# Where the modulation sums, the gate chain and the spatial unit stand in a hybrid transformer layer's projection stage

## Chip, cores, metric

One core of one Trainium2 chip. The metric is the device time of one execution in microseconds (us). Three runs of the kernel before gave a median of 2624.97 us (2623.48 to 2627.48).

## What is computed

One layer on 2048 positions of width 1024, all in float32. Cut to what matters here:

```python
mod = silu(c) @ w_ada + b_ada            # six vectors of 1024
sh1, sc1, gt1, sh2, sc2, gt2 = split(mod)
h = rms_norm(x, g_mix) * (1 + sc1) + sh1
p = h @ w_in                             # q, k, v | qm, km, vm, om | u, v of the spatial unit | gates
y_attn  = forgetting_attention(...)      # 8 heads of 64, q and k normed per head
y_mlstm = mlstm_chunkwise(...)           # 4 heads, log-sigmoid forget gates
y_sgu   = gelu(u) * (tril(w_s) @ layer_norm(gelu(v)) + b_s)   # chunks of 128
x = x + gt1 * (concat(y) @ w_out)
x = x + gt2 * conv_ffn(rms_norm(x, g_ffn) * (1 + sc2) + sh2)
```

sh1 and sc1 are needed at once; sh2, sc2, gt1 and gt2 only when the projection stage is over.

## The kernel before

**Stages.** The projections (h @ w_in with what feeds attention and mLSTM) fill about the first 740 us. Attention, the output projection, and the up and down products of the channel network follow; the change does not touch them.

**Projection stage.** Two halves of 1024 positions, each with seven column blocks in this order: keys of mLSTM with the gates (272 columns), queries and output gates of mLSTM (512), values of mLSTM (256), spatial unit (512), k (512), q (512), v (512). Blocks of 512 columns are called wide (`wide[0]`). A block has eight results of 128 positions (of 512 in the second block, with the operands changed over). A result has eight k-steps, and a k-step three matmuls, since both operands are split in a high and a low part (`mm3`, L53 to L56). So a wide result is 24 matmuls of 512 columns on TensorE (PE).

**Ticks.** `products` (L598) issues the k-steps of a result and calls `tick` at its end, and in wide blocks also behind its fourth k-step. `tick` (L624) does what stands due: jobs that `after(n, f)` put off by n ticks; one step of `chores[0]`; one step of `background[0]`. The written order of these calls isn't quite that of the engines' queues: the layer that builds the program places each engine's instructions by estimates of its own, so the fences under the change show the order as it was built.

**Modulation sums.** `rest_of_mod` (L449), the only chore, makes the eight remaining column blocks of `mod` in 64 steps. A step multiplies a 128x512 tile of w_ada (`wa`) by a column of silu(c) and adds it to `modacc` on VectorE (DVE; L466 for the first of eight, L468 for the others). Its tile is loaded by a DMA on the queue of SyncE (SP), two steps ahead. The tiles lie in a ring of four buffers (tag t2k), which the bias row, the gate rows and h32 share. After the eighth step `columns_or_row` sums over partitions on PE, either by a matmul with 512 columns (L482) or by four with one column (L488), into the one bank of `misc_ps`. With a step at each tick from the second block on, the 64 steps are done in the k block of half 0.

**Weights.** The next block's eight weight tiles (`wr`, ring of four) are loaded on SP's queue and split by ScalarE (ACT, L592 for the high part) and DVE (L593 for the low part) during the present block.

**Gate chain.** `log_gates` (L796) turns the gates into logarithms: DVE, two activations on ACT (L803, L804, each behind a load of its function table), DVE (L805, L806). `rows(qi)` (L857), two for each half in the background, turns them over on PE (L868) and makes the rows that mLSTM and attention need.

**Spatial unit.** After four results of its block, `spatial` (L725) calls `mix(0)` to `mix(3)`, a matmul (L732) and two operations of DVE (L733, L734) each, two a tick, and then `turn(0)` and `turn(1)`, four transpositions each (L741). Their results go by turns to the one bank of `misc_ps` (called mp in the profile) and to the ring of two banks of `tr_ps` (trp). Also in mp: the key transpositions of mLSTM (L960, copied by ACT at L962) and the modulation sums (L482, L488). Also in trp: the transpositions of q and k (L781), and of h (L557).

**k and q.** `use_qk` squares a result on ACT, sums on DVE (L767, L768), takes the reciprocal root on GpSimd (POOL, L128), scales on DVE (L773) and turns over on PE three ticks later (L781).

Of the kernel before, what the change touches and what calls it, by code (L numbers as in the profile page):

```python
# [33 lines left out]
def trunk(  # L34
# [337 lines left out]
    def tr_ps():  # L372
        return pp.tile([P, 512], F32, name="trp", tag="trp")
# [75 lines left out]
    def rest_of_mod():  # L449

        seq = [(col, k) for col in (3072, 3584, 4096, 4608, 2048, 2560, 5120, 5632) for k in range(KT)]
        tiles = {}

        def load(i):
            if i < len(seq):
                col, k = seq[i]
                tiles[i] = pool.tile([P, 512], F32, name="wa", tag="t2k")
                dma(tiles[i], w_ada[k * P : k * P + P, col : col + 512])

        load(0)  # L460
        load(1)
        for i, (col, k) in enumerate(seq):
            st = tiles.pop(i)
            if k == 0:
                acc = pool.tile([P, 512], F32, name="modacc", tag="macc")
                V.tensor_scalar(acc, st, cs[:, 0:1], None, op0=ALU.mult)  # L466
            else:
                V.scalar_tensor_tensor(acc, st, cs[:, k : k + 1], acc, op0=ALU.mult, op1=ALU.add)  # L468
            load(i + 2)
            if k == 6:  # L470
                brow = pool.tile([1, 512], F32, name="brow", tag="t2k")
                dma(brow, b_ada[:, col : col + 512])
            if k == 7:
                V.tensor_tensor(acc[0:1, :], acc[0:1, :], brow, op=ALU.add)
                after(2, lambda acc=acc, col=col: columns_or_row(acc, col))
            yield
# [90 lines left out]
    class Weights:  # L567
# [7 lines left out]
        def load(self):  # L575
            k = len(self.raw)
            if k == KT:
                return
            raw = pool.tile([P, 512], F32, name="wr", tag=self.tags[k])
            o = 0  # L580
            for col, wd in self.parts:
                dma(raw[:, o : o + wd], w_in[k * P : (k + 1) * P, col : col + wd])
                o += wd
            self.raw.append(raw[:, : self.width])
# [13 lines left out]
    def products(i, mm):  # L598

        w = nxt[0]  # L600
        for k in range(KT):
            mm(k)
            if k == 3 and wide[0]:
                tick()
            if w and i == 7:
                if k in (0, 1, 2, 5):
                    w.cast()
                if k in (0, 1):
                    w.load()
        if w and 1 <= i <= 3:  # L610
            w.load()
        if w and 4 <= i <= 6:
            w.cast()
            w.load()
        tick()
# [4 lines left out]
    chores, started = [], []  # L620
    background = []
    ticks = [0]

    def tick():  # L624
        ticks[0] += 1
        due()
        if chores and started and next(chores[0], True):
            chores.pop(0)
        if background and next(background[0], True):
            background.pop(0)  # L630
# [15 lines left out]
    def after(n, f):  # L646

        pending.append((ticks[0] + n, f))
# [76 lines left out]
    def spatial(tt, u, vn):  # L725
        y = pool.tile([P, 4, 256], F32, name="sy", tag="t4k")

        def mix(g):
            sl = slice(g * 64, g * 64 + 64)
            mp = (misc_ps, tr_ps)[g % 2]()  # L730
            m3 = mp[:, 0:256].rearrange("p (n c) -> p n c", n=4)
            T.matmul(m3, wT[:, g, :], vn[:, :, sl], start=True, stop=True)  # L732
            V.tensor_tensor(y[:, :, sl], m3, bc(gsgu[:, sl], 1, 4), op=ALU.mult)  # L733
            V.scalar_tensor_tensor(  # L734
                y[:, :, sl], y[:, :, sl], bs_col[:, g : g + 1], u[:, :, sl], op0=ALU.add, op1=ALU.mult
            )

        def turn(j):
            mp = (misc_ps, tr_ps)[j % 2]()
            for n in range(4):  # L740
                T.transpose(mp[:, n * P : (n + 1) * P], y[:, n, j * P : (j + 1) * P], ident)  # L741
            t5 = pool.tile([P, 512], F32, name="evq", tag="sq")
            A.copy(t5, mp)
            dma(yt_d[768 + j * P : 896 + j * P, (tt - 3) * P : (tt + 1) * P], t5)

        for g in range(4):
            after(g // 2 + 1, lambda g=g: mix(g))
        for j in range(2):
            after(j + 4, lambda j=j: turn(j))
# [105 lines left out]
    cols = {}  # L855

    def rows(qi):  # L857
        t0 = qi * 512
        neb = nebs[qi % 2]
        ra = pool.tile([P, 512], F32, name="ra", tag="ra")  # L860
        rb = pool.tile([P, 512], F32, name="rb", tag="rb")
        r4 = lambda t: t.rearrange("p (n l) -> p n l", l=P)

        psG = mps()
        g = gates[:, qi // 2].rearrange("p a n h -> p (a n h)")
        for i in range(4):
            o = (qi % 2 * 4 + i) * 4
            T.transpose(psG[0:100, i * P : (i + 1) * P], g[:, o : o + 100], ident)  # L868
        psI = psG[64:68, :]
        m, e, lf = ra[0:4], ra[32:36], ra[64:68]  # L870
        b, a, ne = rb[0:4], rb[32:36], rb[64:68]
        V.tensor_copy(lf, psG[96:100, :])
        mp_ = pool.tile([36, 5], F32, name="mprev", tag="mprev")[32:36]
        V.tensor_copy(mp_[:, 0:1], mcar)
        yield
        V.tensor_tensor_scan(m, lf, psI, mcar, op0=ALU.add, op1=ALU.max)
        V.tensor_tensor_scan(b, rmask, lf, 0.0, op0=ALU.mult, op1=ALU.add)
        V.tensor_copy(mp_[:, 1:5], r4(m)[:, :, P - 1])
        V.tensor_copy(mcar, mp_[:, 4:5])
        yield  # L880
        V.tensor_tensor(a, psI, b, op=ALU.subtract)
        V.tensor_tensor(e, m, b, op=ALU.subtract)
        V.tensor_scalar(R[32:36], m, -1.0, None, op0=ALU.mult)
        V.tensor_copy(R[96:100], a)
        yield
        V.tensor_tensor(r4(R[0:4]), bc(mp_[:, 0:4], 2, P), r4(e), op=ALU.subtract)
        V.tensor_tensor(r4(R[64:68]), r4(a), r4(e)[:, :, P - 1 : P].broadcast_to([4, 4, P]), op=ALU.subtract)
        V.tensor_tensor(dec[0:4], mp_[:, 0:4], r4(e)[:, :, P - 1], op=ALU.subtract)
        yield
        fr = pool.tile([P, 512], F32, name="fr", tag="macc")  # L890
        for r in (0, 32):
            V.tensor_tensor_scan(
                fr[r : r + 4], ones[r : r + 4, 0:1].broadcast_to([4, 512]), psG[r : r + 4, :], fc[r : r + 4],
                op0=ALU.mult, op1=ALU.add,
            )
            V.tensor_copy(fc[r : r + 4], fr[r : r + 4, 511:512])
            dma(nf_d[r // 8 : r // 8 + 4, t0 : t0 + 512], fr[r : r + 4])
        yield
        psR = mps()
        for i in range(4):  # L900
            T.transpose(psR[:, i * P : i * P + 100], R[0:100, i * P : (i + 1) * P], ident[0:100, 0:100])
        psD = misc_ps()
        for pr in range(2):
            T.matmul(psD[:, pr * 4 : pr * 4 + 4], sel[:, pr, :], dec, start=True, stop=True)
        V.tensor_scalar(neb[32:36], e, -1.0, None, op0=ALU.mult)
        V.scalar_tensor_tensor(ne, e, -1.0, neb[32:36], op0=ALU.mult, op1=ALU.subtract)
        yield
        psR4 = psR.rearrange("p (n l) -> p n l", l=P)
        ecol = pool.tile([P, 4, 68], F32, name="ecol", tag="ecol")
        A.activation(ecol, psR4[:, :, 0:68], AF.Exp)  # L910
        acol = pool.tile([P, 4, 4], F32, name="acol", tag="acol")
        V.tensor_copy(acol, psR4[:, :, 96:100])
        dcol = pool.tile([P, 2, 4], F32, name="dcol", tag="dcol")
        A.activation(dcol.rearrange("p a b -> p (a b)"), psD[:, 0:8], AF.Exp)
        V.tensor_copy(neb[64:68], ne)
        V.tensor_tensor(neb[96:100], ne, neb[64:68], op=ALU.subtract)
        cols[qi] = ecol, acol, dcol
# [264 lines left out]
    class Block:  # L1182
# [10 lines left out]
        def mm(self, i, nb):  # L1193
            if i not in self.x:
                self.x[i] = pool.tile([P, D], F32, name="x2")
                dma(self.x[i], x[self.rows(i), :])
                self.st[i] = pool.tile([P, 2], F32, name="st", tag="wst_")
            sl = slice(i * P, (i + 1) * P)
            ps = self.ps[i, nb] = pp.tile([P, 512], F32, name="wps")
            for k in range(KT):  # L1200
                mm3(ps, self.y[k][0][:, sl], self.y[k][1][:, sl], *wo[nb * 8 + k], k == 0, k == KT - 1)
# [534 lines left out]
```

## Time and profile before

| | us |
|---|---|
| median of the runs | 2624.97 |
| the profiled execution's own time | 2626.13 |
| its span in the trace | 2624.1 |
| PE busy | 2537.4 (97%) |
| DVE busy | 2004.4 (76%) |
| ACT busy | 1274.2 (49%) |
| PE's granted clock, mean | 0.992 |

A row of the waits gives the engine, the operation that waited, what it waited for, the total in us, how often, and the longest. A row of a timeline gives start, duration, engine, line, operation, tiles, shape, and in brackets the idle time in front of it with what ended it. A row of the stretches gives from:to, length, busy us of PE, of PE's weight loads, DVE, ACT and POOL (with the number of instructions), PE's granted clock, the share of the DMA engines and GB/s. A group row has count, busy time and mean ns, and behind the last bar the idle time before the group's instructions.

### The profile page before, as it was taken

What the parts mean: (1) busy time and instruction counts of PE and PEld (TensorE: products, weight loads), DVE (VectorE), ACT (ScalarE), POOL (GpSimd) and SP (SyncE); (2) the same over time, 40 slices, a digit from 0 to 9 for tenths busy, and PEclk for the clock granted to TensorE, in tenths of its full rate; (3) what the DMA queues carried; (4) which work ended last, traced back from release to release, by engine and by line L of the source; (5) the groups of instructions that cost most, each with busy time, mean ns of one, the idle gap of its engine ahead of it and who ended that gap; (6) DMA issues with size and microseconds to landing.
All of it is one profiled execution on the core that took longest, in us unless ns stands there. A gap on an engine that the chain in (4) does not pass through costs nothing.

```text
span 2624.1 us, 36472 instructions
## 1 busy us (share of the span) xinstructions
PE 2537.4 (97%) x12521; PEld 2101.5 (80%) x12537; DVE 2004.4 (76%) x3438; ACT 1274.2 (49%) x2424; POOL 399.0 (15%) x532
## 2 busy tenths in 40 slices
PE   5999999999999999999989999999999999999999
PEld 4887878878787887777768888888888888888787
DVE  7856646455378888866769888888888887898797
ACT  4333334333278888854555444444444444444443
POOL 2012210032246656620000000000000000000000
PEclk9999999999999999999999999999999999999999
DMA  7564653334564445257723222246222227658533
GB/s 248 173 185 132 194 153 111 116 88 131 165 177 113 114 136 165 65 162 238 274 65 105 89 81 84 86 160 225 81 88 81 87 66 256 233 166 295 186 95 117
DMA packets 302592, 379.58 MB, mean 145 GB/s; under 512 B 31934, under 2 KB 194588, under 8 KB 300360
## 3 DMA queue, kind: packets, MB, share of 16 engines
q1 hardware_dynamic: 302408, 377.26, 45.4%
q8 instruction: 99, 1.62, 0.3%
q14 instruction: 85, 0.70, 0.1%
HBM read 276.44 MB, written 100.74 MB: 144 GB/s over the span
## 4 chain that ended last, share of the span: by engine, by line
PE 76%; DVE 10%; DMA 5%; ACT 3%; issue 3%; POOL 2%; SPq 1%; DVEq 0%; ACTq 0%; POOLq 0%
PE ub L56 10%; PE ub L55 10%; PE ub L54 10%; PE acc L54 5%; PE acc L56 5%; PE acc L55 5%; PE db L55 4%; PE db L56 4%; PE db L54 4%; PE sp L206 3%; PE tp L259 3%; PE wps L55 2%; PE wps L54 2%; PE wps L56 2%; PE op L245 2%
## 5 line engine op out<-in xcount | busy, mean ns | idle before, releaser
L54 PE MATMUL acc<-wh,hh 128*128 128x512 f32 (+2 forms) x768 | 288.2, 376 | 4.3 <-DVE ev L688 2.3
L54 PE MATMUL ub<-T,wsph 128*128 128x512 f32 x704 | 274.2, 390 | 5.8 <-ACT wsph L1348 5.8
L56 PE MATMUL acc<-wh,hl 128*128 128x512 f32 (+2 forms) x768 | 275.7, 362 | 0.8 <-DVE hl L563 0.5
L55 PE MATMUL acc<-wl,hh 128*128 128x512 f32 (+2 forms) x768 | 275.3, 360 | 0.3 <-DVE wl L593 0.3
L56 PE MATMUL ub<-T,wspl 128*128 128x512 f32 x704 | 273.7, 389 | 0.6 <-DVE wspl L1349 0.6
L55 PE MATMUL ub<-T,wsph 128*128 128x512 f32 x704 | 273.9, 389 | 0.0
L55 PE MATMUL db<-wspl,wsph 128*128 128x512 f32 x616 | 240.2, 390 | 2.6 <-DVE wspl L1480 2.6
L56 PE MATMUL db<-wsph,wspl 128*128 128x512 f32 x616 | 239.6, 389 | 0.0
L54 PE MATMUL db<-wsph 128*128 128x512 f32 x616 | 238.2, 389 | 0.3 <-ACT wsph L1479 0.3
L1348 ACT CAST wsph<-S 128x512 fp32r<-128x512 f32 x176 | 109.7, 623 | 227.7 <-PE ub L55 159.1
L263 DVE TENSOR_TENSOR plo<-tp,phi 128x512 fp32r<-128x512 f32 (+1 forms) x320 | 186.9, 607 | 31.6 <-ACT phi L262 29.4
L54 PE MATMUL ub<-B,wsph 128*128 128x512 f32 x528 | 207.1, 392 | 2.8 <-ACT wsph L1348 2.8
L56 PE MATMUL ub<-B,wspl 128*128 128x512 f32 x528 | 207.0, 392 | 0.7 <-DVE wspl L1349 0.7
L55 PE MATMUL ub<-B,wsph 128*128 128x512 f32 x528 | 206.8, 392 | 0.0
L223 ACT ACTIVATE L<-L,nm 128x1024 f32<-128x1024 f32 (+2 forms) x192 | 172.5, 902 | 35.7 <-DVE nm L212 34.4
L259 PE MATMUL tp<-ident,L 128*128 128x128 f32 x1088 | 177.0, 274 | 2.6 <-POOL L L228 0.8
L262 ACT CAST phi<-tp 128x512 fp32r<-128x512 f32 (+1 forms) x320 | 159.9, 520 | 40.5 <-PE tp L259 38.9
L206 PE MATMUL sp<-kk,q 128*128 128x512 f32 (+3 forms) x640 | 169.3, 375 | 3.2 <-DVE nm L212 2.2
L1479 ACT CAST wsph<-act 128x512 fp32r<-128x512 f32 x132 | 82.2, 623 | 178.9 <-PE db L55 161.0
L228 POOL TENSOR_SCALAR L<-L,rs 128x1024 f32<-128x1024 f32 (+2 forms) x192 | 167.2, 880 | 11.0
L54 PEld LDWEIGHTS acc<-wh,hh 128*128 128x128 f32 x768 | 147.1, 192 | 24.2 <-DVE ev L688 2.7
L56 PEld LDWEIGHTS acc<-wh,hl 128*128 128x128 f32 x768 | 146.0, 191 | 23.1 <-DVE hl L563 1.3
(339 smaller groups left out, 5936.2 us busy)
## 6 DMA issues: line engine op xcount, KB each, us to landing
w<-in_w_up_dram SPq DMA_DIRECT2D x88, 512.0 KB
wd<-in_w_down_dram SPq DMA_DIRECT2D x176, 256.0 KB
wa<-in_w_ada_dram SPq DMA_DIRECT2D x96, 256.0 KB
act_d<-yc SPq DMA_DIRECT2D x44, 512.0 KB
act<-act_d SPq DMA_DIRECT2D x44, 512.0 KB
wr<-in_w_in_dram SPq DMA_DIRECT2D x64, 256.0 KB
q<-q_d SPq DMA_DIRECT2D x128, 128.0 KB
hc_d<-hl SPq DMA_DIRECT2D x28, 512.0 KB
```

Of the source, the lines that this page charges most:

```text
L54: T.matmul(ps, lh, rh, start=start, stop=False, skip_group_check=resume)
L55: T.matmul(ps, lh, rl, start=False, stop=False, skip_group_check=resume)
L56: T.matmul(ps, ll, rh, start=False, stop=stop, skip_group_check=resume)
L206: T.matmul(sp[:, b : b + bw], q2[n][:, qs], kk[:, s0 + b : s0 + b + bw], start=n == 0, stop=n == 1 and not last)
L223: A.activation(L[c], L[c], AF.Exp, bias=nm[:, n - 1 : n], scale=-1.0, accum_out=rs[:, c : c + 1])
L228: G.tensor_scalar(t, t, rs[:, 0:1], 1.0, op0=ALU.mult, op1=ALU.mult)
L245: T.matmul(op[:, c0:], vv[:, j, :], hi[:, c0:], start=(j == 0), stop=False)
L259: T.transpose(tp[:, i * P : (i + 1) * P], rows[i][j // 8][:, (j % 8) * P : (j % 8 + 1) * P], ident)
L262: A.copy(hi[:, c0:], tp[:, c0:])
L263: V.tensor_tensor(lo[:, c0:], tp[:, c0:], hi[:, c0:].bitcast(F32), op=ALU.subtract)
L1348: A.copy(hi, src)
L1479: A.copy(hi, v)
```

## The change

Four parts. (1) The sums advance only at the tick in the middle of a wide result: one step a result instead of two, none in narrow blocks, so that the 64 steps end in the k block of half 1. Their tiles are loaded one step ahead instead of two. (2) The next block's first four weight tiles are loaded from result 0 on instead of from result 1, and one load of the last result falls away. (3) `rows(0)` and `rows(2)`, the first of each half, begin two ticks later. (4) `mix` and `turn` take all banks from `tr_ps`.

```diff
         load(0)
-        load(1)
         for i, (col, k) in enumerate(seq):
...
-            load(i + 2)
+            load(i + 1)
...
             if k == 3 and wide[0]:
-                tick()
+                tick(True)
             if w and i == 7:
                 if k in (0, 1, 2, 5):
                     w.cast()
-                if k in (0, 1):
+                if k == 0:
                     w.load()
-        if w and 1 <= i <= 3:
+        if w and i <= 3:
             w.load()
...
-    def tick():
+    def tick(middle=False):
         ticks[0] += 1
         due()
-        if chores and started and next(chores[0], True):
+        if middle and chores and started and next(chores[0], True):
             chores.pop(0)
...
         def mix(g):
-            mp = (misc_ps, tr_ps)[g % 2]()
+            mp = tr_ps()
...
         def turn(j):
-            mp = (misc_ps, tr_ps)[j % 2]()
+            mp = tr_ps()
...
     def rows(qi):
+        if qi % 2 == 0:
+            yield
+            yield
```

Line numbers in the changed kernel are one less than before from L462 to L856 and two more behind that.

PE's queue around the first transposition of the gates (L868, in the changed kernel L870), second block of half 0. acc_985 is the bank of the block's first result, the next acc that of the second; hh_480 belongs to the fourth of the eight k-steps, hh_524 to the last. Before:

```order
L54 MATMUL acc_985<-hh_524,wh_973 128x512
L868 MATMUL mps_1008<-ident_74,gates_85 100x128 x4
L55 MATMUL acc_985<-hl_525,wh_973 128x512
L56 MATMUL acc_985<-hh_524,wl_974 128x512
L54 MATMUL acc_1038<-hh_447,wh_839 128x512
```

Of the change:

```order
L54 MATMUL acc_1021<-hh_480,wh_929 128x512
L55 MATMUL acc_1021<-hl_481,wh_929 128x512
L56 MATMUL acc_1021<-hh_480,wl_930 128x512
L870 MATMUL mps_1039<-ident_74,gates_85 100x128 x4
L54 MATMUL acc_1021<-hh_491,wh_939 128x512
```

The transposition stood in the last k-step of the first result and stands behind the fourth k-step of the second, 14 matmuls later. In half 1 it moves by 24.

DVE's queue at the beginning of the k block of half 1, where the spatial unit's second group of four results is mixed (sy is its result; mp and trp are the banks; L767 to L773 belong to k's norm). Before:

```order
L767 TENSOR_REDUCE ss_5770<-qsq_5768 128x8
L768 TENSOR_SCALAR ss_5770<-ss_5770 128x8
L773 TENSOR_TENSOR qn_5788<-acc_5722,ss_5770 128x512
L733 TENSOR_TENSOR sy_5787<-mp_5804,gsgu_279 128x4x64
L767 TENSOR_REDUCE ss_5833<-qsq_5831 128x8
L734 TENSOR_SCALAR sy_5787<-sy_5787,colA_86,su_5485 128x4x64
L733 TENSOR_TENSOR sy_5787<-trp_5808,gsgu_279 128x4x64
```

Of the change:

```order
L467 TENSOR_SCALAR modacc_5708<-wa_5710,cs_92,modacc_5708 128x512
L766 TENSOR_REDUCE ss_5745<-qsq_5743 128x8
L767 TENSOR_SCALAR ss_5745<-ss_5745 128x8
L772 TENSOR_TENSOR qn_5763<-acc_5686,ss_5745 128x512
L467 TENSOR_SCALAR modacc_5708<-wa_5766,cs_92,modacc_5708 128x512
L467 TENSOR_SCALAR modacc_5708<-wa_5839,cs_92,modacc_5708 128x512
L467 TENSOR_SCALAR modacc_5708<-wa_5917,cs_92,modacc_5708 128x512
L467 TENSOR_SCALAR modacc_5708<-wa_6008,cs_92,modacc_5708 128x512
L732 TENSOR_TENSOR sy_5762<-trp_5782,gsgu_279 128x4x64
L766 TENSOR_REDUCE ss_5811<-qsq_5809 128x8
L733 TENSOR_SCALAR sy_5762<-sy_5762,colA_86,su_5439 128x4x64
L732 TENSOR_TENSOR sy_5762<-trp_5786,gsgu_279 128x4x64
```

Four sums have come between the scaled k and the first mix. At the same place of half 0 four sums stood there before, and three stand there now.

PE's queue in the spatial unit's block of half 0, where mLSTM's scores begin (mps is the bank of the scores). Before:

```order
L56 MATMUL acc_1745<-wh_1741,hl_525 128x512
L981 MATMUL mps_1801<-qz0_295,kT_1736 128x256
L488 MATMUL mp_1790<-ones_83,modacc_1440 128x1 x4
L981 MATMUL mps_1801<-qz0_295,kT_1736 128x256
L983 MATMUL mps_1802<-Cst_320,qT_1665 128x130 x2
```

Of the change:

```order
L56 MATMUL acc_1681<-wh_1677,hl_525 128x512
L983 MATMUL mps_1730<-qz0_295,kT_1672 128x256 x2
L985 MATMUL mps_1731<-Cst_320,qT_1607 128x130 x2
L54 MATMUL acc_1751<-wh_1530,hh_447 128x512
L55 MATMUL acc_1751<-wl_1531,hh_447 128x512
```

The sum's four matmuls into mp no longer stand there.

## Prediction

> **What bounds the kernel now.** The page's busy line, its row of granted clock and its chain of waits come first.
>
> ```profile
> PE 2537.4 (97%) x12521; PEld 2101.5 (80%) x12537; DVE 2004.4 (76%) x3438; ACT 1274.2 (49%) x2424; POOL 399.0 (15%) x532
> PE 76%; DVE 10%; DMA 5%; ACT 3%; issue 3%; POOL 2%; SPq 1%; DVEq 0%; ACTq 0%; POOLq 0%
> ```
>
> TensorE (PE) is busy for 2537.4 of 2624.1 us, so nothing in VectorE (DVE), ScalarE (ACT) or the queues counts unless PE stops for it. The change adds and removes no matmul. It can only move the time in which PE stands idle, or runs slowly, in the projection stage (0 to about 740 us). So the second view is PE's own waits in that stage; these rows lie where the change can reach (us in total, times, longest).
>
> ```profile
> PE mps L868 <- DVE gates L806: 5.2, 2, 2.8
> PE mp L732 <- DVE sy L733: 4.7, 1, 4.7
> PE mp L960 <- DVE sy L733: 3.1, 2, 2.8
> ...
> PE trp L557 <- ACT h L561: 3.0, 1, 3.0
> PE acc L54 <- DVE ev L688: 2.3, 2, 1.3
> ...
> PE mp L488 <- ACT kT L962: 2.0, 1, 2.0
> ...
> PE acc L55 <- DVE wl L593: 0.3, 1, 0.3
> ```
>
> That is 20.6 us in ten waits, 0.8% of the kernel: a ceiling of what idle time alone can give back. PE's timeline says where they are and what follows them (start, duration, matmul, idle time before it). I call the places A to F.
>
> ```profile
> 82.09 0.39 PE L54 MATMUL acc<-hh,wh 128*128 128x512 f32 x1
> 85.28 0.81 PE L868 MATMUL mps<-ident,gates 128*100 128x128 f32 x4 [2.80 <-DVE gates L806]
> ...
> 86.74 0.63 PE L54 MATMUL acc<-hh,wh 128*128 128x512 f32 x1
> 87.16 0.63 PE L55 MATMUL acc<-hl,wh 128*128 128x512 f32 x1
> ...
> 165.31 1.05 PE L488 MATMUL mp<-ones,modacc 128*128 128x1 f32 x8 [1.97 <-ACT kT L962]
> ...
> 238.00 0.39 PE L55 MATMUL acc<-wl,hh 128*128 128x512 f32 x1
> 238.23 0.39 PE L56 MATMUL acc<-wh,hl 128*128 128x512 f32 x1
> 243.29 1.22 PE L732 MATMUL mp<-sv,wT 128*128 128x256 f32 x2 [4.68 <-DVE sy L733]
> ...
> 394.16 0.66 PE L557 MATMUL trp<-ident,xt 128*128 128x128 f32 x4 [3.01 <-ACT h L561]
> ...
> 432.55 0.64 PE L868 MATMUL mps<-ident,gates 128*100 128x128 f32 x4 [2.41 <-DVE gates L806]
> ...
> 577.24 0.59 PE L732 MATMUL mp<-sv,wT 128*128 128x256 f32 x2
> ...
> 581.32 0.69 PE L960 MATMUL mp<-ident,kn 128*128 128x128 f32 x2 [2.83 <-DVE sy L733]
> ```
>
> A is 85.28, B 165.31, C 243.29, D 394.16, E 432.55, F 581.32. Look at the starts: before C two matmuls lie 0.23 us apart, behind A they lie 0.42 us apart. PE runs at about half speed after a wait, so a wait costs more than its idle time. The stretches give the price (length, busy times, granted clock, DMA share, GB/s):
>
> ```profile
> 85.00:90.00 5.00, 4.72 (x16) 3.87 (x17) 4.59 (x9) 1.04 (x3) 0.00 (x0) 0.66 0.45 136
> 165.00:170.00 5.00, 4.69 (x22) 4.04 (x23) 3.55 (x10) 2.70 (x5) 0.00 (x0) 0.75 0.26 81
> 170.00:175.00 5.00, 5.00 (x28) 4.30 (x27) 3.01 (x11) 0.00 (x0) 2.59 (x3) 0.90 0.74 236
> 243.00:250.00 7.00, 6.46 (x17) 4.73 (x18) 6.89 (x16) 0.37 (x1) 1.80 (x1) 0.54 0.50 167
> 394.00:404.00 10.00, 9.84 (x79) 9.66 (x80) 9.86 (x22) 8.56 (x17) 0.00 (x0) 1.00 0.75 244
> 434.00:444.00 10.00, 10.00 (x39) 8.06 (x39) 9.71 (x17) 1.20 (x2) 0.00 (x0) 0.84 0.19 60
> 580.00:590.00 10.00, 8.62 (x32) 7.03 (x34) 3.65 (x8) 3.37 (x6) 1.01 (x2) 0.66 0.13 35
> ```
>
> Lost to the clock, as (1 - clock) times length: A 0.34 x 5 = 1.7 us; B 0.25 x 5 + 0.10 x 5 = 1.75; C 0.46 x 7 = 3.2; D none; E 0.16 x 10 = 1.6; F 0.34 x 10 = 3.4, of which I take 2.6, since 1.3 us of the wait lie in the window. With its wait each place costs: A 4.5, B 3.7, C 4.7 + 0.25 + 3.2 = 8.1, D 3.0, E 4.0, F 5.4. Together 28.7 us.
>
> The Trainium skill, page "TensorE: Matmul & The Clock Gate", section "Part 1: The HAM clock gate", says that the clock halves after at least one idle window of about 3.4 us, and that the windows run freely. By that rule only C's 4.68 us would surely cost clock, and the sum below would be 5.05 us smaller (A, B and E without their 1.7, 1.75 and 1.6). The trace speaks against it: slow matmuls follow waits of 1.97 and 2.80 us, and none follow D's 3.01.
>
> **The change part by part.**
>
> *Gate chain later (A and E).* L868 turns the gates over after DVE's L806, which ends this chain:
>
> ```profile
> 80.87 0.75 ACT L592 CAST wh<-wr 128x256 fp32r<-128x256 f32 x2 [2.96 <-DMA wr<-in_w_in_dram]
> 81.64 1.28 ACT L803 ACT_TABLE_LOAD   x1
> ...
> 84.89 0.22 DVE L805 TENSOR_TENSOR gates<-lg,lg 128x64 f32<-128x64 f32 x1 [1.90 <-ACT lg L804]
> ```
>
> The order moves L868 in half 0 from behind the first matmul of the last k-step of a result to the middle of the next: 14 matmuls later, 14 x 0.227 = 3.2 us against the wait of 2.80. A goes: -4.5. If the chain itself slides by a cast (0.4 us), nothing changes; if the sums now ahead of it on DVE add two operations of 0.75, 1.1 us stay and the clock may with them (-1.7). In half 1 it moves 24 matmuls, 5.4 us against 2.41; the sums that now stand near L805 cost about 2.2 us (three of 0.75), and 5.4 still covers 4.6: -4.0. Bound: 0, if a sum waits for its tile there.
>
> *Sums at half rate (B).* L488 at B needs the one bank mp, which waits for L962's copy on ACT. In the new order no sum's matmul stands between the key transposes and the score matmuls there, and the other L488 and L482 have the bank free for many matmuls: -3.7. Bounds -3.7 and 0 (the score matmul L981 reads the same copy, so it may wait in its place).
>
> *Spatial unit in transposition banks, with the sums beside it (C and F).* Mixes 0 and 1 take the two trp banks, mixes 2 and 3 need them back, so now mix 2 waits for L733 of mix 0, and mix 3 for L733 of mix 1. DVE's rows at C and F:
>
> ```profile
> 236.15 0.69 DVE L773 TENSOR_TENSOR qn<-acc,ss 128x512 f32<-128x512 f32 x1 [1.75 <-POOL ss L128]
> 238.44 2.33 DVE L468 SCALAR_TENSOR_TENSOR modacc<-wa,cs,modacc 128x512 f32<-128x512 f32 x3 [1.60 <-DMA wa<-in_w_ada_dram]
> 242.15 0.75 DVE L468 SCALAR_TENSOR_TENSOR modacc<-wa,cs,modacc 128x512 f32<-128x512 f32 x1 [1.39 <-DMA wa<-in_w_ada_dram]
> 242.82 0.42 DVE L733 TENSOR_TENSOR sy<-mp,gsgu 128x256 f32<-128x256 f32 x1
> ...
> 575.86 0.69 DVE L773 TENSOR_TENSOR qn<-acc,ss 128x512 f32<-128x512 f32 x1 [1.75 <-POOL ss L128]
> 576.47 0.41 DVE L733 TENSOR_TENSOR sy<-mp,gsgu 128x256 f32<-128x256 f32 x1
> ```
>
> At C four sums stand between L773 (done 236.84) and L733, two of them late by their DMA. After the change three stand there. Three take 2.33; with one late tile of 1.60, L733 runs from 240.8 to 241.2. PE is ready at 243.29 - 4.68 = 238.6: mix 2 waits 2.6. L733 of mix 1 comes behind one L767 (0.68), one L734 (0.43) and itself (0.41), at 242.7, and mix 3 waits 1.1 more. So 3.7 us idle where 4.93 were. For the clock I take 2.4, in proportion (3.2 x 3.7 / 4.93): 6.1 against 8.1, or -2.0. Bounds: -8.1 if no wait is left, +2 with two late tiles.
>
> F has no sums before the change. After it, four stand between L773 (done 576.55) and L733: 4 x 0.777 = 3.1, so L733 ends at 580.1. Mix 2 is due at 577.24 and waits 2.8; mix 3 waits 1.1: 3.9 against 2.83, the clock as before: +1.1. L960 has bank mp to itself and waits no more. I take no late tile: there are four buffers, and the first of these sums stands ahead of L767 in the new order, so that the fifth tile can be on its way some 5 us (573.2 to 578.9, three sums behind L773) before it is needed. Bounds -5.4, and +2 x 1.6 more with two late tiles: +4.3.
>
> *Weights one result sooner.* The waits of PE for weights are 0.3 us in all, and those for the eviction L688, held behind casts, 2.3 in two: -1.0 (bounds -1.3, and +2.0 if the earlier load holds up a sum's tile on the one DMA queue, SP's, by 1.6). At D one matmul of a sum, about 0.9 us, now stands where PE was idle, and has left another place: -0.9 (0 to -3.0).
>
> *Sums in new places.* Forty of the 64 steps now run in half 0's q and v and half 1's blocks. This group row tells what they cost DVE:
>
> ```profile
> L468 DVE SCALAR_TENSOR_TENSOR modacc<-wa,cs,modacc 128x512 f32<-128x512 f32 x55 | 41.2, 749 | 16.0 <-DMA wa<-in_w_ada_dram 14.9 <-DVE modacc L468 0.3
> ```
>
> They waited 14.9 us for tiles and only at C did PE notice. I take +1.5, one small new wait (0 to +8).
>
> **Sum:** -4.5 - 4.0 - 3.7 - 2.0 + 1.1 - 1.0 - 0.9 + 1.5 = -13.5. The profiled execution took 2626.13 us (span and 2.03 around it): 2612.6. The median of the runs shown, 2624.97, lies 1.2 lower, so the median forecast is 2624.97 - 13.5 = 2611.5. The rivals are taken from the median too.
>
> **The rivals.** *All waits go:* if DVE reaches L733 in time at C and F as well, A, B, C, E and F go whole, and D and the weights by 1.9: 25.7 + 1.9 = 27.6 less, or 2597.4; with half a place and one small new wait left (2.0 + 1.5), about 2601. For it: at F L733 of mix 0 is in time today. Against: the order puts sums there.
>
> *The waits move:* the sums in half 1 hold L805 and E stays (+4.0), C and F each get one more late tile with its clock (+2.4 and +1.6), B's bank wait passes to L981 for half its price (+1.9): -13.5 + 9.9 = -3.6, or 2621.4. For it: L468 waits for tiles today with two loads ahead. Against: at half rate one load ahead is the same time, 24 x 0.227 = 5.4 us, as two at full rate.
>
> *Slower, by late tiles ahead of reads:* DVE works in order, so a sum that waits for its tile holds every read of a PSUM bank behind it. Each such place costs a wait of 1.6 and some 2.0 of clock, 3.6. The trace shows it at C with two tiles; if it happened at six places in the wide blocks of half 1, where no sum stood, it gives -13.5 + 6 x 3.6 = +8.1: 2633.1. It decides for slower by over 0.2% from about 5.2 places on (18.7 / 3.6). For it: four buffers are shared with other users. Against: of the sums in the group row above, all but the two at C held nobody.
>
> *It does nothing at L868:* if the chain of logs moves with it, A and E stay (+8.5): -5.0, or 2620.0.
>
> **How the numbers follow.** Forecast (2605 to 2619) 0.51; all waits go 0.14; the waits move, or L868 keeps them, 0.20; slower 0.15. A measurement of this kernel tells about 0.2%, 5.2 us, from no change, so the third case counts as same: faster 0.65, same 0.20, slower 0.15. The range, 2600 to 2630, leaves out about 0.05 below and 0.13 above.
>
> **What would show it.** Right: no wait of L868 for L806, no wait of L488 for L962, clock 1.00 around these; at C and F waits of 2 to 4 us on L733 under trp and none under mp. Wrong: DVE waits of L468 for wa ahead of L805 or L733 in half 1, new slow stretches in half 1, or slow clock without waits.

## The result and the profile after

| | before | after |
|---|---|---|
| median, us (22 runs each) | 2625.25 (2618.39 to 2628.99) | 2620.31 (2615.23 to 2625.63) |
| ratio | | 0.9982, 95% interval 0.9974 to 0.9989 |
| span of the profiled execution | 2624.1 | 2622.1 |

The change makes the kernel 4.9 us faster, 0.18%. The forecast was 13.5 us: right in sign, but not in size. Two rivals' numbers, 2621.4 (the waits move) and 2620.0 (L868 keeps its waits), lie close to the measured 2620.31, but neither tells what happened: both left a gate wait standing, and both are gone.

The waits of PE (TensorE) in the projection stage of the changed kernel, the rows that answer to those of before:

```profile
PE trp L731 <- DVE sy L732: 7.4, 2, 4.0
...
PE mps L985 <- ACT M L940: 4.6, 1, 4.6
...
PE mp L506 <- DVE colC L507: 2.7, 1, 2.7
...
PE trp L556 <- ACT h L560: 0.9, 1, 0.9
```

The two waits for the gates are gone, and so are those of the evictions, of the casts and of bank mp (L488 and L960). Two rows are new: L985, mLSTM's second group of scores, waits 4.6 us for its decay rows (M), and L506, a transposition in `small_setup`, waits 2.7 us for DVE's copy L507. The timeline has the places:

```profile
86.49 0.60 PE L870 MATMUL mps<-ident,gates 128*100 128x128 f32 x4
...
160.43 1.24 PE L985 MATMUL mps<-Cst,qT 128*128 128x130 f32 x4 [4.56 <-ACT M L940]
...
235.72 2.54 PE L731 MATMUL trp<-sv,wT 128*128 128x256 f32 x4 [3.38 <-DVE sy L732]
...
384.89 1.33 PE L556 MATMUL trp<-ident,xt 128*128 128x128 f32 x8 [0.85 <-ACT h L560]
...
493.08 0.30 PE L506 MATMUL mp<-ident,crow 88*128 88x88 f32 x1 [2.67 <-DVE colC L507]
...
574.25 2.54 PE L731 MATMUL trp<-sv,wT 128*128 128x256 f32 x4 [4.01 <-DVE sy L732]
```

The granted clock (the figure behind POOL's) is 1.00 where the gates are turned over, and low behind the new waits as behind the old ones:

```profile
82.00:87.00 5.00, 5.00 (x26) 4.15 (x25) 3.72 (x9) 4.54 (x8) 0.00 (x0) 1.00 0.64 190
160.00:167.00 7.00, 6.57 (x23) 5.52 (x23) 3.76 (x9) 3.09 (x7) 1.96 (x2) 0.57 0.45 136
235.00:242.00 7.00, 6.18 (x16) 4.43 (x17) 5.85 (x14) 0.37 (x1) 2.07 (x1) 0.56 0.62 200
...
493.00:498.00 5.00, 4.92 (x19) 3.71 (x20) 2.35 (x5) 2.84 (x4) 0.00 (x0) 0.66 0.91 301
574.00:581.00 7.00, 6.65 (x21) 4.88 (x22) 5.87 (x14) 0.46 (x2) 2.07 (x1) 0.64 0.47 154
```

A sharper measure than the whole time is where the stage ends. One row of the view of L206, attention's score matmul, gives its first start, first for the kernel before, then for the changed one:

```profile
L206 PE MATMUL sp<-kk,q x640: 218/393/504, 694.7 to 1134.0; 128*128 128x512 f32 x127, 128*128 128x128 f32 x17, 128*128 128x384 f32 x16
```

```profile
L206 PE MATMUL sp<-kk,q x640: 218/393/505, 689.3 to 1130.0; 128*128 128x512 f32 x127, 128*128 128x128 f32 x17, 128*128 128x384 f32 x16
```

The stage ends 5.4 us sooner, which agrees with the medians. The starts of PE's first matmul in each block, taken from the timelines, divide these 5.4 us (each step is the change of the difference from the mark before):

| mark (first matmul) | before | after | difference | step | what lies in it |
|---|---|---|---|---|---|
| first block | 41.6 | 42.0 | +0.4 | +0.4 | |
| second block, half 0 | 77.3 | 78.3 | +1.0 | +0.6 | |
| 256-column block | 129.1 | 124.5 | -4.6 | -5.6 | A, gates |
| spatial unit's block | 156.5 | 148.6 | -7.9 | -3.3 | evictions, casts |
| mix 0 in the k block | 234.8 | 228.6 | -6.3 | +1.6 | B, first scores |
| first block, half 1 | 394.6 | 386.0 | -8.6 | -2.3 | C, mixes; D |
| second block, half 1 | 427.2 | 418.6 | -8.6 | 0.0 | |
| 256-column block | 477.6 | 464.9 | -12.8 | -4.2 | E, gates |
| spatial unit's block | 500.8 | 488.9 | -11.9 | +0.9 | |
| mix 0 in the k block | 573.6 | 566.4 | -7.2 | +4.7 | L506, small setup |
| first L206 | 694.7 | 689.3 | -5.4 | +1.8 | F, mixes |

At the 256-column block of half 1 the changed kernel is 12.8 us ahead, nearly the whole forecast. It had won 7.9 by the first spatial block and lost 1.6 at B, and in half 1 it loses 7.4 from there to the end. The steps hold more than waits: matmuls of sums that have moved from one block to another count in them too.

At C and F one wait is left at each place, that of mix 2. DVE's rows there, in the changed kernel:

```profile
232.41 0.69 DVE L772 TENSOR_TENSOR qn<-acc,ss 128x512 f32<-128x512 f32 x1 [1.53 <-POOL ss L128]
233.02 2.32 DVE L467 SCALAR_TENSOR_TENSOR modacc<-wa,cs,modacc 128x512 f32<-128x512 f32 x3
235.25 0.42 DVE L732 TENSOR_TENSOR sy<-trp,gsgu 128x256 f32<-128x256 f32 x1
...
569.48 0.69 DVE L772 TENSOR_TENSOR qn<-acc,ss 128x512 f32<-128x512 f32 x1 [1.75 <-POOL ss L128]
570.09 0.75 DVE L467 SCALAR_TENSOR_TENSOR modacc<-wa,cs,modacc 128x512 f32<-128x512 f32 x1
571.54 2.33 DVE L467 SCALAR_TENSOR_TENSOR modacc<-wa,cs,modacc 128x512 f32<-128x512 f32 x3 [0.71 <-DMA wa<-in_w_ada_dram]
```

At C none of the three sums is late, at F one is, by 0.71 us.

### Why the decay rows are late

PE waits at B for M, which ACT makes behind the casts of raw weights. Three views of the changed kernel follow that wait back: ACT, then DVE, then SP's queue.

```profile
155.56 1.35 ACT L591 CAST wh<-wr 128x512 fp32r<-128x512 f32 x2 [6.36 <-DMA wr<-in_w_in_dram]
157.31 0.62 ACT L591 CAST wh<-wr 128x512 fp32r<-128x512 f32 x1 [0.39 <-DMA wr<-in_w_in_dram]
157.94 1.28 ACT L940 ACT_TABLE_LOAD   x1
```

```profile
139.58 0.75 DVE L467 SCALAR_TENSOR_TENSOR modacc<-wa,cs,modacc 128x512 f32<-128x512 f32 x1 [4.95 <-DMA wa<-in_w_ada_dram]
...
142.09 1.54 DVE L467 SCALAR_TENSOR_TENSOR modacc<-wa,cs,modacc 128x512 f32<-128x512 f32 x2 [1.42 <-DMA wa<-in_w_ada_dram]
...
148.56 0.68 DVE L473 TENSOR_TENSOR modacc<-modacc,brow 1x512 f32<-1x512 f32 x1
149.16 0.41 DVE L687 COPY ev<-acc 128x256 f32<-128x256 f32 x1
149.50 2.48 DVE L592 TENSOR_TENSOR wl<-wr,wh 128x512 fp32r<-128x512 f32 x4
```

```profile
148.26 2.07 SPq L458 DMA_DIRECT2D wa<-in_w_ada_dram  x3
...
150.86 1.85 SPq L581 DMA_DIRECT2D wr<-in_w_in_dram  x2
...
153.29 0.38 SPq L581 DMA_DIRECT2D wr<-in_w_in_dram  x1
```

Put in order of time: a whole set of eight sums stands on DVE in the 256-column block (133 to 149 us), where the source has none; the builder placed the k block's set there. It waits 4.95 and 1.42 us for tiles, and the low casts L592 stand behind it (149.50). They are the last readers of the raw weights in four buffers, so the loads of the next ones start at 150.86, ACT's casts wait for them until 155.56, and M comes behind them. None of these steps waits for PE in the rows shown, so PE's being early should not hasten them; the runs below test that.

The same shape stands at the small setup, on DVE: a sum (L465) waits for its tile, then come an eviction, four low casts and another eviction, and L507 last, while PE waits for it.

```profile
489.31 0.49 DVE L465 TENSOR_SCALAR modacc<-wa,cs 128x512 f32<-128x512 f32 x1 [0.95 <-DMA wa<-in_w_ada_dram]
...
490.04 2.49 DVE L592 TENSOR_TENSOR wl<-wr,wh 128x512 fp32r<-128x512 f32 x4
492.45 0.42 DVE L687 COPY ev<-acc 128x256 f32<-128x256 f32 x1
492.78 0.24 DVE L507 COPY colC<-mp 128x88 f32<-128x88 f32 x1
```

### The profile page after: what moved, and what is told of

The parts are those of the page before. It is cut to its first block, busy times and chain, and to the rows that moved or that the text cites. A ratio compares the mean times of both kernels' runs of the same rounds, so it can differ in the third digit from the quotient of the medians.

```text
span 2622.1 us, 36482 instructions
## 1 busy us (share of the span) xinstructions
PE 2537.9 (97%) x12537; PEld 2102.2 (80%) x12537; DVE 2003.8 (76%) x3438; ACT 1274.6 (49%) x2424; POOL 398.3 (15%) x532
## 3 DMA queue, kind: packets, MB, share of 16 engines
q8 instruction: 99, 1.62, 0.3%
## 4 chain that ended last, share of the span: by engine, by line
PE 77%; DVE 10%; DMA 6%; issue 3%; ACT 2%; POOL 2%; SPq 0%; DVEq 0%; ACTq 0%; POOLq 0%
PE ub L56 11%; PE ub L55 10%; PE ub L54 10%; PE acc L54 5%; PE acc L56 5%; PE acc L55 5%; PE db L55 4%; PE db L56 4%; PE db L54 4%; PE sp L206 3%; PE tp L259 3%; PE op L245 2%; PE op L246 2%; PE wps L56 2%; PE wps L55 2%
## 5 line engine op out<-in xcount | busy, mean ns | idle before, releaser
L206 PE MATMUL sp<-kk,q 128*128 128x512 f32 (+3 forms) x640 | 169.3, 375 | 3.4 <-DVE nm L212 2.4
```

What stands on the lines that cost most here:

```text
L206: T.matmul(sp[:, b : b + bw], q2[n][:, qs], kk[:, s0 + b : s0 + b + bw], start=n == 0, stop=n == 1 and not last)
```

## The experiments

Each ran with runs of the kernel before on the same chip; ratios are against those. "Stage end" is the first start of L206. The rest of the program is the same in all and took 1928.9 to 1933.6 us in the twelve profiles, so a single profile's total carries about 2 us that don't come from the stage. A stage end, too, is that of one profile: slow stretches that cost 1.7 or 3.4 us come at one place in one profile and not in the next (last section), so a difference of 2 to 3 us between two stage ends can be that alone.

### The four parts one at a time

Gate chain later, alone:

```diff
     def rows(qi):
+        if qi % 2 == 0:
+            yield
+            yield
```

> Part 3 alone on the kernel before (gate chain two ticks later). Both theories: no wait at the two transpositions of the gates, worth 4.5 and 4.0 us. Theory (the sums lose): the wait at the first scores stays near 2 us, first score matmul of attention at 685 to 687, time 8 to 10 us faster. Rival (PE comes earlier and waits at the scores instead): the wait at the scores rises to 4 to 7 us, first score matmul at 689 to 692, time 3 to 6 us faster.

Measured: 2623.89 us, ratio 0.9995 (0.9987 to 1.0004); stage end 690.8. Both gate waits are gone, and the wait at the scores has risen from 1.97 to 6.27:

```profile
165.37 1.87 PE L488 MATMUL mp<-ones,modacc 128*128 128x1 f32 x8 [6.27 <-ACT kT L965]
```

PE's start after the wait, 165.37, is within 0.1 us of the 165.31 of before: what was won ahead of it is waited away. The time is one that PE can't hurry. This was the rival's outcome in waits and stage end (PE comes earlier and waits), with 3.9 us won at the stage's end, mostly at E. The median fell by only 1.6 us, less than either theory gave.

Everything but the sums' part (parts 2, 3 and 4; part 1 undone):

```diff
-        if middle and chores and started and next(chores[0], True):
+        if chores and started and next(chores[0], True):
...
+        load(1)
...
-            load(i + 1)
+            load(i + 2)
```

> The change without part 1: sums at every tick with tiles two steps ahead as before, weights sooner, gate chain later, banks of the spatial unit changed. Theory (the sums lose): waits of the gates gone, the wait at the first mLSTM scores 2 us or less, none at the small setup, first score matmul of attention at 682 to 687 (changed kernel 689.3), time 9 to 13 us faster than before. Rival (PE merely comes earlier): the wait at the scores is 4 us or more here too, first score matmul at 688 to 692, time 3 to 6 us faster than before.

Measured: 2617.81 us, ratio 0.9972 (0.9961 to 0.9983); stage end 687.7, within neither range (the theory's ended at 687, the rival's began at 688). My theory fell here: with the sums as before, the wait at the scores is the longest of all.

```profile
163.57 1.66 PE L488 MATMUL mp<-ones,modacc 128*128 128x1 f32 x7 [6.82 <-ACT kT L965]
```

So the half rate isn't needed for the wait at the scores. The small setup has no wait in this run, but PE also gets there 9.7 us later than in the changed kernel (498.6 against 488.9 at the block's start), so this run alone doesn't say which of the two took it away.

The sums' part alone:

```diff
-        if chores and started and next(chores[0], True):
+        if middle and chores and started and next(chores[0], True):
...
-        load(1)
...
-            load(i + 2)
+            load(i + 1)
```

> Part 1 alone on the kernel before (sums at half rate, tiles one step ahead). Theory (the sums lose what the other parts win: steps written for the next wide block are placed in the 256-column block ahead of it, where DVE waits for their tiles and holds up the low casts, the weight loads and with them ACT's decay rows): PE's wait at the first mLSTM scores stays or grows (2 to 5 us), a wait appears at the small setup's second transposition (2 to 3 us), both gate waits stay; the first score matmul of attention, at 694.7 us in the kernel before, comes between 693 and 699, time within 0.2% of before or up to 4 us slower. Rival (the wait at the scores grows only because PE comes there earlier when the gate wait is gone): the wait at the scores is 2 us or less, first score matmul at 689 to 692, time 3 to 6 us faster.

Measured: 2627.01 us, ratio 1.0006 (0.9998 to 1.0015); stage end 692.0. Against the theory, the wait at the scores is 0.75 and there is none at the small setup. PE comes there 3 us later than in the changed kernel (492.0 against 488.9 at the block's start), since the gate waits stay (1.51 and 3.19), while DVE's copy L507 starts at nearly the same time (493.10 against 492.78). So the wait at the small setup needs PE's being early. That it needs the sums in the 256-column block too is shown by the runs below with the sums tied elsewhere, in which PE comes earlier still (480.2 to 486.9) and doesn't wait there. At both k blocks mixes wait, in half 1 for 4.00 and then 2.23 us where 2.83 were. Half rate by itself wins nothing that can be measured in the median.

The spatial unit's banks alone:

```diff
-            mp = (misc_ps, tr_ps)[g % 2]()
+            mp = tr_ps()
...
-            mp = (misc_ps, tr_ps)[j % 2]()
+            mp = tr_ps()
```

> Part 4 alone on the kernel before (spatial unit in the two transposition banks only). In half 1 no sum stands ahead of the mixes, so their third and fourth should wait 1 to 3 us where 2.8 were waited at the key transpositions; in half 0 four sums still stand there and 4 to 5 us of wait stay. First score matmul of attention at 692 to 696, time within 3 us of before. A rival, that the change of bank is itself the loss at the spatial unit (mixes waiting for each other rather than for sums), gives over 4 us of wait at both places and 697 or later.

Measured: 2621.19 us, ratio 0.9982 (0.9974 to 0.999); stage end 687.1, earlier than expected, and the median is 4.3 us faster where at most 3 were. In half 1, with no sum ahead of the mixes, the wait falls from 2.83 to 0.43 and no slow stretch follows:

```profile
575.82 0.70 PE L732 MATMUL trp<-sv,wT 128*128 128x256 f32 x2 [0.43 <-DVE sy L733]
```

In half 0, behind four sums, 4.40 remain. So the bank was the cause at F and the sums are the cause at C. By the ratios this part alone wins as much as the whole change. Not all of the 7.6 us at the stage's end is its own: the waits at B and E, which it doesn't touch, are followed by no slow stretch in this profile and that at D is, a net 1.7 us.

Weights one result sooner, alone:

```diff
-                if k in (0, 1):
+                if k == 0:
...
-        if w and 1 <= i <= 3:
+        if w and i <= 3:
```

> Part 2 alone on the kernel before (weights one result sooner). Forecast in the prediction: 1 us. The waits of the evictions and casts in the 256-column block (2.6 us in three) go or halve, the rest stays; first score matmul of attention at 691 to 695, time within 0.2% of before.

Measured: 2624.13 us, ratio 0.9995 (0.9987 to 1.0004); stage end 690.3, 0.7 us beyond the early end of what was expected; no slow stretch follows the waits at E and F in this profile, and the median is 0.8 us faster. The waits of evictions and casts fall from 2.6 to 1.4 us. The one of the scores is still there (1.73).

### Where the sums stand

The runs above left two explanations of the time of M: the sums in the 256-column block, or ACT's casts themselves, which wait until PE has left the old weights. To take the sums out of that block against the builder's placing, each set of eight is tied to a value of the block where it shall stand; adding zero times a finite value leaves the factors as they are. The steps were written for the k block from its fourth result on, and for q and v (q alone in half 1), two a wide result:

```diff
+                cg = cgs[i // KT]
+                V.scalar_tensor_tensor(cg, anchor[0], 0.0, cs, op0=ALU.mult, op1=ALU.add)
-                V.tensor_scalar(acc, st, cs[:, 0:1], None, op0=ALU.mult)
+                V.tensor_scalar(acc, st, cg[:, 0:1], None, op0=ALU.mult)
...
+            anchor[0] = ss
```

On the kernel before, with nothing else changed:

> The kernel before with only its sums held to those places. Theory (sums in the 256-column block): the wait of 2.0 at the scores goes, the 4.7 us of the spatial unit in half 0 fall to 3 or less, the gate waits of 2.8 and 2.4 stay or grow by up to 1; first score matmul of attention at 683 to 688, time 6 to 12 us faster. Rival (casts behind PE): the wait at the scores stays at 2 or grows by what PE comes earlier; first score matmul at 687 to 692.

Measured: 2619.96 us, ratio 0.9979 (0.997 to 0.9988); stage end 685.5. The median is 5.0 us faster, less than the 6 to 12 expected, while the stage end is as expected. The wait at the scores is 0.73, and PE gets to that place 8 us earlier than before, so that the casts-behind-PE rival is out. The first gate wait falls from 2.80 to 1.09; in the kernel before, sums stood on DVE there too, but this wasn't tried by itself.

With the gate chain later as well:

> The kernel before with its sums held to those places and the gate chain two ticks later, banks and weights as before. Theory (sums in the 256-column block): against the run with sums held alone both gate waits go and nothing takes their place at the scores (wait 1 us or less): first score matmul of attention 7 to 9 us earlier than there. Rival (casts behind PE): the gain of the first gate wait is lost at the scores (wait 4 to 7), only 3 to 5 us earlier.

Measured: 2614.7 us, ratio 0.9956 (0.9943 to 0.9969); stage end 678.7, 6.8 us earlier than with the sums late alone. Both gate waits are gone and the scores wait 0.86. Slightly under the 7 to 9 expected, because the first gate wait was only 1.09 by then. Against 3.9 in the gates-only run, the same edit is worth nearly twice as much once the sums have left.

The changed kernel with its sums late (two steps a wide result, tiles two ahead):

> The changed kernel with its sums held to other places: written for the second part of each k block and for the q and v blocks, two steps a wide result, tiles two ahead, and each set of eight tied by its data (silu(c) plus zero times a value of the block) so that the builder can't place it earlier. Theory (sums placed in the 256-column block wait there for their tiles, hold DVE's low casts, so the weight loads, ACT's casts and the decay rows come at a time that PE can't hurry): no wait over 1 us at the first mLSTM scores or at the small setup, spatial unit's waits 1 us or less, both gate waits gone; first score matmul of attention at 668 to 675 (changed kernel 689.3, before 694.7), time 18 to 26 us faster than before. Rival (ACT's casts wait for PE to leave the old weights, and the decay rows come behind them whatever the sums do): the wait at the scores stays at 4 to 7 us in half 0, first score matmul at 677 to 684, time 10 to 16 us faster.

Measured: 2605.79 us, ratio 0.9927 (0.9915 to 0.9939); stage end 673.2. This beats both kernels: before by 19.2 us on the same chip, the changed one by 14.5 by its median above.

```profile
156.50 0.71 PE L996 MATMUL mps<-Cst,qT 128*128 128x130 f32 x4 [1.29 <-ACT M L951]
...
226.01 0.70 PE L740 MATMUL trp<-sv,wT 128*128 128x256 f32 x2 [0.42 <-DVE sy L741]
```

The scores wait 1.29, a little more than the 1 us expected, the mixes 0.42 in both halves, the small setup not at all. Besides the placing, this run differs from the changed kernel in the rate (two steps a result) and the loads (two ahead); the next run keeps both.

The half rate of the change kept, but each set tied to the block that the source names, so that none can slip into the 256-column block:

```diff
-        if middle and chores and started and next(chores[0], True):
+        if (middle and at[0] >= 1 or not middle and wide[0] and at[0] == 7) and chores and started and next(chores[0], True):
...
+        anchor[0] = t[:, 0, 0:8]
```

> The changed kernel with its half rate kept as it is written: each set of eight sums tied by its data to the wide block it is written for (second queries, spatial unit, k, q, v and so on), one step a result, so that the builder can't place a set in the 256-column block ahead. Theory (the sets placed in the 256-column blocks make the waits at the first scores and at the small setup): the wait of 4.6 at the scores falls to 2 or less and the 2.7 at the small setup goes; the waits of the spatial unit, where the k block's set still stands, stay at 2 to 5 us; first score matmul of attention at 678 to 684 (changed kernel 689.3, all sums late 673.2), time 10 to 15 us faster than before. Rival (half rate itself is too dense in the wide blocks, wherever the builder puts it): the wait at the scores stays over 3 and the first score matmul at 686 or later.

Measured: 2613.72 us, ratio 0.9957 (0.9945 to 0.997); stage end 679.5. Rate and loads are those of the changed kernel and only the placing differs, and the two new waits go; those of the mixes, where the k block's set still stands, remain:

```profile
157.01 0.71 PE L995 MATMUL mps<-Cst,qT 128*128 128x130 f32 x4 [0.60 <-ACT M L950]
...
565.41 2.08 PE L739 MATMUL trp<-sv,wT 128*128 128x256 f32 x4 [4.92 <-DVE sy L740]
```

Last, the best version with five buffers of raw weights and three for the sums' ring:

```diff
-        ("wr", 2048, 4)
+        ("wr", 2048, 5)
-        ("t2k", 2048, 4)
+        ("t2k", 2048, 3)
```

> The changed kernel with all sums late (second part of k, q and v blocks) and one more buffer for raw weights (five), one less for the ring of the sums (three). If the wait of 1.3 us that is left at the first scores comes from raw weights that wait for a free buffer, it falls below 0.6 and the first score matmul of attention comes 1 to 2 us before the 673.2 of the run with four buffers; time 0 to 3 us below its 2605.8. If it comes from ACT's casts and table loads alone, it stays at 1.0 to 1.5. The shorter ring of the sums can cost up to 3 us in the first 40 us, where the first modulation sums run.

Measured: 2606.21 us, ratio 0.9928 (0.9914 to 0.9941); stage end 671.7, 1.5 earlier, but the scores still wait 1.32. So the 1.3 us left there don't come from that buffer, and the time is not better.

## Why the prediction was wrong in size

- **Gates (A and E, -4.5 and -4.0): right where they stand.** -5.6 and -4.2 by the marks, and the clock is 1.00 there. Of the -5.6, about 1.0 is a sum's eight matmuls that have left this block; 4.5 is the wait with its slow stretch.
- **B (-3.7): wrong, and the step that failed.** I priced the wait as a conflict over bank mp, which goes when the sum's matmuls leave. The text had the other end: "the score matmul L981 reads the same copy, so it may wait in its place". So it was, and worse: the copy and the decay rows come at a time set by sums on DVE, low casts, weight loads and ACT's casts. A term that PE wins upstream is lost again there. The place gave +1.6, 5.3 us off, and even that flatters it: the wait rose from 1.97 to 4.56 us and the slow windows of 3.41 us behind it from one to two, some 3.6 us lost, while ten of the sums' matmuls, nearly 2 us, left this stretch for others. The gates-only run shows it alone (165.37 against 165.31), and the runs with the sums tied elsewhere show its cause.
- **Sums in new places (+1.5): mis-sized.** The small setup's wait of 2.67 and its slow stretch (0.34 x 5 = 1.7) are 4.4 of the 4.7 us lost in that stretch of half 1. I had asked only which wide blocks the sums enter, and had read the built order at three places; the set in the 256-column block stood in it, plain to see. Nor was it true of the kernel before that of its sums "all but the two at C held nobody": there, too, a sum in the 256-column block waited for its tile, 4.28 us, with an eviction behind it for which PE waited. And tying the sums elsewhere in that kernel brought PE to the scores 8 us sooner. (Its last sums stand at 314 to 319 us, in half 0's q block, not in the k block.)

```profile
148.55 1.54 DVE L468 SCALAR_TENSOR_TENSOR modacc<-wa,cs,modacc 128x512 f32<-128x512 f32 x2 [4.28 <-DMA wa<-in_w_ada_dram]
150.00 0.42 DVE L688 COPY ev<-acc 128x256 f32<-128x256 f32 x1
```

```profile
150.47 0.39 PE L54 MATMUL acc<-wh,hh 128*128 128x256 f32 x1 [1.35 <-DVE ev L688]
```

- **C (-2.0), D (-0.9) and F (+1.1): near in size, at C and F partly by luck.** C and D give -2.3 together against -2.9, F +1.8. The wait of 1.1 us foreseen for mix 3 came at neither place, and mix 2 waited longer: 3.38 for 2.6 at C, 4.01 for 2.8 at F. At C I took one tile 1.60 late and none was; but k's norm stands behind sums as well, so the scaled k (L772) starts 3.85 us behind mix 0 (232.41 against 228.56), where it was 1.32 before (236.15 against 234.83). At F there was one late tile (0.71 us) where I took none. That the sums, not the banks, make these waits is shown by the runs: 0.42 us without sums, 0.43 with the banks alone in half 1.
- **Weights and evictions (-1.0): too small.** -3.3 in half 0's 256-column block; the eviction waits (2.3) and the cast wait (0.3) all went, and the other 0.7 is no wait and stays open. The weights alone left 1.4 of 2.6, so half of it comes from elsewhere. I had put the eviction waits down to casts; the longer one, 1.35 us, stood behind the late sum of the rows above.
- **The clock: read from too few rows.** I took each place's slow stretch in one profile for its price, and D's full clock after 3.01 us as evidence against a rule. Over the twelve profiles the place doesn't decide it: E kept full clock after 2.07, 2.53 and 2.56 us in three runs, and D had a slow stretch in six of nine with a wait over 2 us (last section). Nor would C's wait of 4.68 us "surely" hold a whole window of 3.41 us wherever the windows lie; that takes twice 3.41. In this profile it does, from 239.2 to 242.6. Some 5.9 of the forecast's 13.5 us were slow stretches that would go (A 1.7, B 1.75, C 0.8, E 1.6). From 60 us to the stage's end both profiles have seven slow windows of 3.41 us; those of A and E went, and others came at B and at the small setup. PE's idle time in the same stretch fell from 22.1 to 17.5 us, which is most of what the change won.

By size: -13.5 plus 5.3 (B) plus 3.2 (small setup: 4.7 for 1.5) plus 1.0 (the first two marks, not explained) plus 0.9 (half 1's 256-column block, where one matmul of a sum now stands) plus 0.6 (C and D) plus 0.7 (F), less 1.1 and 0.2 (A and E) and 2.3 (evictions), is -5.4, the measured stage.

## What to carry to other kernels

Before adding up waits that an edit removes, follow each later wait back to see whether it ends at a time that moves with the waiting engine or at one set by a chain on other engines; gains ahead of the second kind vanish. Filler work is placed in an engine's queue by the builder, not by the line where it is written: read the built order for all of it, and where it must stay out of a block, tie it by data. Here, tying the sums to the blocks that the source names made the change worth 11 us instead of 5; placing them later still, at two a result, made it 19.

## What the runs showed of the hardware

From the length of a wait alone, one can't tell between about 1.7 and 3.4 us whether PE slows down after it. Counted over the twelve profiles, between 60 us and the end of the projection stage: of 19 waits from 1.0 to 1.72 us none was followed by a slow stretch; of two of 1.73 us one was; of the 30 from 1.9 to 3.4 us 21 were; of the 13 longer ones all were (a stretch counts as slow where the granted clock of the 7 us behind the wait is under 0.93). The same wait of 2.83 us at half 1's k block stands in the next two rows, first the weights-only run, then the kernel before, each from the end of the wait (the figure behind POOL's is the clock):

```profile
579.00:585.00 6.00, 5.29 (x30) 4.44 (x31) 3.19 (x8) 2.63 (x4) 0.14 (x1) 1.00 0.09 28
```

```profile
581.00:588.00 7.00, 6.62 (x24) 5.37 (x25) 2.01 (x5) 1.40 (x3) 0.00 (x0) 0.54 0.07 19
```

And D, where the forecast had argued from 1.00, in the run of the banks alone (wait 3.07) and in the changed kernel with its sums late (2.94):

```profile
392.40:400.00 7.60, 7.60 (x51) 7.54 (x52) 6.97 (x15) 6.57 (x11) 0.00 (x0) 0.78 0.52 156
```

```profile
376.50:384.00 7.50, 7.43 (x48) 7.18 (x49) 7.35 (x15) 5.30 (x10) 0.00 (x0) 0.77 0.70 207
```

What decides is where the wait lies. The slow stretches of the twelve profiles between 60 us and the end of the stage last 3.41, 6.83 or 10.24 us at a clock of 0.50, and in each profile all their starts and ends lie on one grid of 3.413 us. Cut into the windows of that grid, the same time holds 30 windows at full clock in which PE was idle for 1.94 us or more: a slow window followed each of them. Of the 7 with 1.72 to 1.90 us idle two were so followed, of the 2098 with less one (B in the kernel before, 1.18 us, with eight one-column matmuls in it). The two waits of 2.83 us differ in just this. In the kernel before, 2.05 us of idle time fall into one window, and the next is slow; in the weights-only run 1.62 and 1.21 us fall into two, and neither is followed by a slow one.

```profile
577.13:580.55 3.42, 1.37 (x7) 0.83 (x5) 1.89 (x6) 0.00 (x0) 1.86 (x1) 1.00 0.39 123
580.55:583.96 3.41, 2.64 (x8) 2.16 (x9) 1.83 (x5) 0.37 (x1) 0.00 (x0) 0.50 0.15 38
```

```profile
575.09:578.50 3.41, 1.79 (x9) 1.17 (x7) 2.01 (x6) 0.00 (x0) 1.76 (x1) 1.00 0.16 60
578.50:581.92 3.42, 2.21 (x11) 1.87 (x12) 2.14 (x5) 0.38 (x1) 0.09 (x1) 1.00 0.12 38
```

The grid lies differently in each profile (its first mark stands 0.15 to 3.41 us behind the start of the span), so a forecast can't know it.

The Trainium skill, page "TensorE: Matmul & The Clock Gate", section "Part 1: The HAM clock gate", says that the windows of about 3.4 us run freely and that the clock halves after at least one idle one. The trace agrees with the grid, and with six windows idle from end to end that were each followed by a slow one; that 1.94 us of idle time in a window can suffice goes beyond the words of the rule. A wait between 2 and 3.4 us should therefore be priced with about two thirds of a slow stretch (20 of the 29 counted here had one), not with the one that a single profile happens to show. A stretch of one window costs 1.7 us, half of 3.41.
